# A decoder layer in split float32: one-hot gate rows built four tokens at a time, ScalarE scaling them, and three moves around it

## The chip, the core and the metric

The kernel runs on one core of a Trainium2 chip. A core has five engines that run side by side and hand tiles to each other by semaphores: TensorE (matmul, PE in the profile), VectorE (DVE), ScalarE (ACT), GpSimd (POOL) and SyncE (SP), which here issues most transfers. Each engine takes its instructions in the order in which they are written for it. The metric is the device time of one execution in microseconds; the time stated for a kernel is the median of its runs.

## The reference, cut to what matters

One decoder layer on 512 tokens of 2048 numbers: a projection, two kinds of windowed attention that are merged, a layer norm, then a product-key lookup (PEER) over 128 x 128 single-neuron experts, and a gated extra input.

```python
h1 = layer_norm(alpha * x + m @ w_out)
# PEER: 8 heads; each takes the 16 best of 128 x 128 experts by two half keys,
# expert index = i1 * 128 + i2, gate = softmax of the 16 scores
peer = sum over heads and picks of gate * gelu(h1 . u[expert]) * v[expert]
x = layer_norm(alpha * h1 + peer + sigmoid(h1 @ ple_gate) * (p @ ple_proj))
```

## The kernel before, in words

Every float32 matmul is made of three: operands are split into a rounded high half and a remainder, and `mm3` (lines 100 to 103) multiplies high by high, high by low and low by high. `load_split` (lines 87 to 98) brings in a weight chunk of 128 x 1024: SyncE loads `raw`, ScalarE copies the high half `whi` (line 93), VectorE subtracts to get the low half `wlo` (line 95; in places GpSimd, line 97). Each of the three has three buffers, and so the loads run at most three chunks ahead.

The order of the instructions on each engine is set when the kernel is built: a scheduler simulates the engines and emits what it believes to be ready first, within the dependencies and the buffers of each pool.

The stages that the change touches, in order:

- **Output projection and norm** (`mix`, line 459; `norm1`, line 483; driver, lines 515 to 523). `mix(0)` and `mix(1)` project two halves of 256 tokens, 32 steps each of 12 matmuls of 512 columns (`wo`). After four steps of `mix(1)` the norm of the first half, `norm1(0)`, is written in one piece: statistics, then 16 blocks in four groups, each block two transposes on TensorE (`ht`), a scaling on VectorE (line 502), a high half on ScalarE and a low half `m_lo` on VectorE (line 505). `spread` (lines 509 to 513) then lets GpSimd multiply and add the norm's weights over whole rows, in place, for the tiles `h1g` and `y1` that the transposes read.
- **Key search** (`half_keys`, line 635), interleaved with u columns (`dense_u`, line 712): 48 matmuls of 352 columns each (`hp`), a GELU, and a store to the DRAM tensor `ad`. 32 such columns (four groups of 8 experts) are made early by `look_units` (line 724).
- **Gates** (`dense_gates`, lines 654 to 679). For 352 tokens a 128 x 128 table of gates is the product of two one-hot matrices: VectorE compares an iota with the token's 16 x 8 first indices (`o1`, line 669) and second indices, scaled by the gate (`o2`, line 671), one token at a time; TensorE multiplies them into `pg` (line 673), ScalarE copies four tokens' result to `sg` (line 677), and `gd` in DRAM receives it. After each two groups of four tokens, a **step** (44 in all), `fill(1)` places one unit of other work: the last four u columns of the first 24, then 32 units of the extra input's gate (`ple_units`, line 681; 24 matmuls of 512 columns, chunk names `pg0_0` and so on). `gather_to` places the expert rows' work for the tokens done sparsely: a gather by GpSimd (line 599) and a row step on VectorE (line 606). The unit that closes each quarter of the extra input puts sigmoids into `psg` (line 706) and stores them to `base` by GpSimd's queue.
- **Eight more u columns**, then **gated groups** (loop at line 859). For the first four groups each of 8 values `a` (128 x 352) is loaded from `ad` by GpSimd's queue (line 866), multiplied by the gates `gl` (line 870), split into `ah` (line 873) and `al` (line 874) and used in 48 matmuls `vp`; the value half of the dense experts. Later groups compute `a` in place. The pool of `a` has two buffers.

`raw_p`, a load between key search and gates, holds one of the three `raw` buffers until `pj_lo` (line 781) has read it.

Of the kernel before, what the change touches and what calls it, by code (L numbers as in the profile page):

```python
# [9 lines left out]
F32 = mybir.dt.float32  # L10
# [3 lines left out]
AF = mybir.ActivationFunctionType  # L14
ALU = mybir.AluOpType
# [4 lines left out]
P = 128  # L20
# [7 lines left out]
TD = T - T0  # L28
# [12 lines left out]
def hybrid_layer(  # L41
# [26 lines left out]
    nc = tc.nc  # L68
# [12 lines left out]
    def bank(name, dt=F32):  # L81
        return pp.tile([P, 512], dt, tag="ps", name=name)
# [60 lines left out]
    op = s1.enter_context(tc.tile_pool(name="op", bufs=1))  # L143
# [156 lines left out]
    for c in range(2):  # L300
        ps = column_block(w_z[26 + c], xs, f"vb{c}")
# [181 lines left out]
    def norm1(half):  # L483
        for tb in (2 * half, 2 * half + 1):
            norm_stats(st[:, tb, :, :].rearrange("p a b -> p (a b)"), mv[:, tb, :])
            if tb % 2 == 0:
                nc.vector.tensor_scalar(y[tb], y[tb], mv[:, tb, 0:1], mv[:, tb, 1:2],
                                        op0=ALU.subtract, op1=ALU.mult)
            else:
                nc.vector.scalar_tensor_tensor(mv[:, tb, 2:3], mv[:, tb, 0:1], -1.0, mv[:, tb, 1:2],  # L490
                                               op0=ALU.mult, op1=ALU.mult)
                nc.scalar.activation(y[tb], y[tb], AF.Identity, bias=mv[:, tb, 2:3],
                                     scale=mv[:, tb, 1:2])
        yield
        hc = slice(half * 256, (half + 1) * 256)
        for kb in range(KB):
            ps = bank(f"ht{half}_{kb}")
            for i in range(2):
                nc.tensor.transpose(ps[:, i * P:(i + 1) * P],  # L499
                                    y[2 * half + i][:, kb * P:(kb + 1) * P], ident)  # L500
            t = xp.tile([P, 256], F32, tag="ht", name=f"ht{half}_{kb}")
            nc.vector.tensor_scalar(t, ps[:, 0:256], lnc[:, 0, kb:kb + 1], lnc[:, 1, kb:kb + 1],
                                    op0=ALU.mult, op1=ALU.add)
            nc.scalar.activation(hs[0][:, kb, hc], t, AF.Copy)
            nc.vector.tensor_sub(hs[1][:, kb, hc], t, hs[0][:, kb, hc])
            if kb % 4 == 3:
                yield
# [9 lines left out]
    rest = mix(1)  # L517
    for _ in range(4):
        next(rest)
    for _ in norm1(0):  # L520
        pass
    for _ in rest:
        pass

    pre_q = [load_split(w_q[0][:, u * 1024:(u + 1) * 1024], f"wq0_{u}") for u in range(2)]
# [3 lines left out]
    io = kp.tile([P, P], F32, name="io")  # L529
# [124 lines left out]
    def dense_gates(tb):  # L654
        i1, i2, gt = picks[tb]
        ps = bank(f"pit{tb}")
        for i, a in enumerate((i1, i2, gt)):
            nc.tensor.transpose(ps[:, i * P:(i + 1) * P], a, ident)
        tt = k3.tile([P, 3, P], F32, tag="tt", name=f"tt{tb}", bufs=2)
        nc.vector.tensor_copy(tt, ps[:, 0:384].rearrange("p (a t) -> p a t", t=P))  # L660
        for b in range(GX // 16 if tb == 1 else 0, 8):
            sg = k3.tile([P, P, 16], F32, tag="sg", name=f"sg{tb}_{b}", bufs=2)
            for t4 in range(4):
                ps = bank(f"pg{tb}_{b}_{t4}")
                t0 = b * 16 + t4 * 4
                for t1 in range(4):
                    t = t0 + t1
                    o1 = k3.tile([P, P], F32, tag="o1", name=f"o1_{tb}_{t}", bufs=8)
                    nc.vector.tensor_scalar(o1, io, tt[:, 0, t:t + 1], None, op0=ALU.is_equal)
                    o2 = k3.tile([P, P], F32, tag="o2", name=f"o2_{tb}_{t}", bufs=8)  # L670
                    nc.vector.tensor_scalar(o2, io, tt[:, 1, t:t + 1], tt[:, 2, t:t + 1],
                                            op0=ALU.is_equal, op1=ALU.mult)
                    nc.tensor.matmul(ps[:, t1 * P:(t1 + 1) * P], o1, o2, start=True, stop=True)  # L673
                if t4 % 2:
                    fill(1)
                    gather_to(steps[1] + 1)
                nc.scalar.activation(sg[:, :, t4 * 4:(t4 + 1) * 4].rearrange("p i t -> p t i"),
                                     ps.rearrange("p (t i) -> p t i", i=P), AF.Copy)
            nc.sync.dma_start(gdw[:, :, tb * 8 + b - T0 // 16, :], sg.rearrange("p (g i) t -> p g (i t)", i=GE))
# [43 lines left out]

    def look_units(i, pool, n, share):
        for i2 in range(i, i + n):
            a = pool.tile([P, TD], F32, tag="a", name=f"au{i2}")
            dense_u(i2, a, share())
            nc.sync.dma_start(ad[i2 // GE][:, i2 % GE, :], a)
            yield

    def fill(n):
        for _ in range(n):
            next(units, None)
# [24 lines left out]
    fpool = []  # L758
# [15 lines left out]
    k3 = s4.enter_context(tc.tile_pool(name="k3", bufs=2, side="right"))  # L774
# [8 lines left out]
    def gate_filler():  # L783
        yield from state["units"]
        yield from ple_units()

    units = gate_filler()
    for tb in range(1, NT):
        dense_gates(tb)
    fill(32 + LOOK * GE)  # L790
# [5 lines left out]
    ap2 = s5.enter_context(tc.tile_pool(name="ap2", bufs=2))  # L796
# [3 lines left out]
    def gather_steps():  # L800
        calls[0] += 1
        gather_to(calls[1] + calls[0] * (2 * HG + LEAD - calls[1]) // (NG * 8 + (NG - LOOK + 1) * 8 - 6))
# [56 lines left out]
    for g in range(NG):  # L859
        a_hi, a_lo = [], []  # L860
        if g:
            gt = gate_tile(g)
        for e in range(GE):
            a = ap2.tile([P, TD], F32, tag="a", name=f"a{g}_{e}")
            if g < LOOK:
                nc.gpsimd.dma_start(a, ad[g][:, e, :])
            else:
                dense_u(g * GE + e, a)
            a3 = a.rearrange("p (b t) -> p b t", t=16)
            nc.vector.tensor_mul(a3, a3, gt[:, :, e, :])  # L870
            h = ap2.tile([P, TD], F32R, tag="ah", name=f"ah{g}_{e}", bufs=GE + 1)
            l = ap2.tile([P, TD], F32R, tag="al", name=f"al{g}_{e}", bufs=GE + 1)
            nc.scalar.activation(h, a, AF.Copy)  # L873
            nc.vector.tensor_sub(l, a, h)  # L874
            a_hi.append(h)
            a_lo.append(l)
            if g >= LOOK:
                gather_steps()
        if g == NG - 1:
            lng = gp.tile([P, 2, D], F32, tag="slot_lo", name="lng")  # L880
            nc.sync.dma_start(lng, ln2.partition_broadcast(P))
            zs = gp.tile([P, NT - 1, D], F32, tag="slot_hi", name="zs")
            for tb in range(1, NT):
                lo_, hi_ = span[tb]
                z[tb] = zs[0:hi_ - lo_, tb - 1, :]
                nc.sync.dma_start(z[tb], base[tb][lo_:hi_, :])
        for c in range(8):
            ws = []
            for u in range(GE // 4):
                ws.append(load_split(v_dense[(g * 8 + c) * 2 + u], f"vd{g}_{c}_{u}"))  # L890
            for b in range(2):
                db = c * 2 + b
                ps = bank(f"vp{g}_{db}")
                for e in range(GE):
                    hi, lo = ws[e // 4]
                    o = (e % 4) * 256 + b * P
                    s = slice(o, o + P)
                    mm3(ps[:, :TD], hi[:, s], lo[:, s], a_hi[e], a_lo[e], e == 0, e == GE - 1)
                if g == 0:
                    nc.vector.tensor_copy(acc[:, db, :], ps[:, :TD])  # L900
                else:
                    nc.vector.tensor_add(acc[:, db, :], acc[:, db, :], ps[:, :TD])
            if g == NG - 1 and c % 2:
                for tb in range(1, NT):
                    ps = bank(f"zt{tb}_{c}")
                    lo_, hi_ = span[tb]
                    k = hi_ - lo_
                    for i in range(4):
                        nc.tensor.transpose(ps[:k, i * P:(i + 1) * P],
                                            acc[:, 2 * c - 2 + i, tb * P + lo_ - T0:tb * P + hi_ - T0], ident)  # L910
                    cs = slice(c // 2 * 512, c // 2 * 512 + 512)
                    nc.vector.tensor_add(z[tb][:, cs], z[tb][:, cs], ps[:k, :])
                    nc.vector.bn_stats(st2[:k, tb, c // 2, :], z[tb][:, cs])
            if g == NG - 1 and c >= 3:
                if c == 3:
                    finish_gathered()
            else:
                gather_steps()
# [115 lines left out]
```

## Time and profile before

| | us |
|---|---|
| median of 3 runs | 4023.78 (4021.25 to 4023.92) |
| the profiled execution's own time | 4021.22 |
| its span in the profile | 4019.4 |
| TensorE busy | 3822.7 (95%) |
| VectorE busy | 2704.3 (67%) |
| ScalarE busy | 1282.2 (32%) |
| GpSimd busy | 685.3 (17%) |

The mean granted TensorE clock of this execution is 0.976 of full speed. Matmuls overlap, so their lengths add up to more than the time they take: the distance from one start to the next is the cost. "Idle before" in a group's row is the time its engine stood still just before the group's instructions, and the releaser is what ended it.

### The profile page before, as it was taken

How to read it: one execution, taken by the hardware profiler on the slowest of the kernel's cores; microseconds unless marked ns; L12 is line 12 of the kernel's file. 1: busy time of each engine (PE TensorE's matmuls, PEld its weight loads, DVE VectorE, ACT ScalarE, POOL GpSimd, SP SyncE). 2: the span in 40 equal slices, each digit the busy share in tenths (PEclk: the TensorE clock that was granted, in tenths of full speed). 3: DMA queues.
4: the chain of work that ended last, by engine and by line, in shares of the span. 5: the costliest groups of instructions: out<-in, count | busy, mean ns of one | idle time of the engine just before them, and what ended most of it. 6: DMA issues, size and time to landing. Idle time of an engine off the chain costs nothing.

```text
span 4019.4 us, 54040 instructions
## 1 busy us (share of the span) xinstructions
PE 3822.7 (95%) x21545; PEld 3535.9 (88%) x21545; DVE 2704.3 (67%) x4220; ACT 1282.2 (32%) x1660; POOL 685.3 (17%) x493
## 2 busy tenths in 40 slices
PE   8999999999998889979988899999999999999996
PEld 7888877888886789978878898999999999999996
DVE  5344343222257788899996777777777777777877
ACT  3222233222233433334433222333333333333331
POOL 0000000000002355521122222222211211111110
PEclk9999999999999999989998999999999999999998
DMA  4222222222256455658888787888888888888884
GB/s 141 95 89 85 76 74 71 92 95 94 95 190 191 155 163 181 226 199 281 287 292 303 270 304 287 304 324 310 302 323 303 310 316 298 316 310 306 318 300 152
DMA packets 242941, 886.99 MB, mean 221 GB/s; under 512 B 23040, under 2 KB 76416, under 8 KB 198016
## 3 DMA queue, kind: packets, MB, share of 16 engines
q1 hardware_dynamic: 182672, 499.91, 36.8%
q0 software_dynamic: 52672, 375.15, 25.5%
q10 hardware_dynamic: 7344, 8.47, 0.6%
q8 instruction: 169, 2.77, 0.3%
q14 instruction: 84, 0.69, 0.1%
HBM read 841.24 MB, written 41.42 MB: 220 GB/s over the span
## 4 chain that ended last, share of the span: by engine, by line
PE 81%; DVE 11%; DMA 3%; issue 3%; ACT 1%; POOL 1%; POOLq 0%; DVEq 0%; ACTq 0%; SPq 0%
PE hp L101 8%; PE hp L103 8%; PE hp L102 8%; PE vp L101 7%; PE vp L103 7%; PE vp L102 7%; PE ps_g L101 3%; PE ps_g L102 3%; PE ps_g L103 3%; PE pg L673 2%; DVE row L606 2%; PE pg L101 1%; PE pg L102 1%; PE pg L103 1%; DMA a<-ad 1%
## 5 line engine op out<-in xcount | busy, mean ns | idle before, releaser
L101 PE MATMUL vp<-ah,whi_vd 128*128 128x352 f32 x2048 | 657.5, 327 | 29.1 <-ACT ah L873 18.2
L103 PE MATMUL hp<-m_hi,wlo_u 128*128 128x352 f32 x2048 | 665.2, 325 | 20.4 <-DVE wlo_u L95 13.6
L101 PE MATMUL hp<-m_hi,whi_u 128*128 128x352 f32 x2048 | 668.4, 326 | 0.0
L102 PE MATMUL hp<-m_lo,whi_u 128*128 128x352 f32 x2048 | 662.5, 323 | 0.0
L102 PE MATMUL vp<-al,whi_vd 128*128 128x352 f32 x2048 | 662.1, 325 | 0.3 <-DVE al L874 0.3
L103 PE MATMUL vp<-ah,wlo_vd 128*128 128x352 f32 x2048 | 644.7, 326 | 9.8 <-DVE wlo_vd L95 9.8
L93 ACT ACTIVATE whi_vd<-raw_vd 128x1024 fp32r<-128x1024 f32 x256 | 270.4, 1059 | 671.5 <-PE vp L102 469.7
L93 ACT ACTIVATE whi_u<-raw_u 128x1024 fp32r<-128x1024 f32 x256 | 271.0, 1059 | 525.6 <-PE hp L102 309.1
L101 PEld LDWEIGHTS vp<-ah,whi_vd 128*128 128x128 f32 x2048 | 387.8, 191 | 33.6 <-ACT ah L873 20.1
L95 DVE TENSOR_TENSOR wlo_vd<-raw_vd,whi_vd 128x1024 fp32r<-128x1024 f32 x256 | 312.5, 1221 | 142.6 <-ACT whi_vd L93 142.3
L95 DVE TENSOR_TENSOR wlo_u<-raw_u,whi_u 128x1024 fp32r<-128x1024 f32 x236 | 295.3, 1252 | 165.6 <-ACT whi_u L93 164.9
L103 PEld LDWEIGHTS hp<-m_hi,wlo_u 128*128 128x128 f32 x2048 | 386.3, 189 | 22.4 <-DVE wlo_u L95 15.3
L103 PEld LDWEIGHTS vp<-ah,wlo_vd 128*128 128x128 f32 x2048 | 385.5, 190 | 11.2 <-DVE wlo_vd L95 11.2
L102 PEld LDWEIGHTS hp<-m_lo,whi_u 128*128 128x128 f32 x2048 | 390.1, 190 | 0.0
L102 PEld LDWEIGHTS vp<-al,whi_vd 128*128 128x128 f32 x2048 | 388.4, 190 | 0.9 <-DVE al L874 0.8
L101 PEld LDWEIGHTS hp<-m_hi,whi_u 128*128 128x128 f32 x2048 | 388.0, 189 | 0.0
L599 POOL DMA_INDIRECT row<-in_u_rows,eidx x160 | 204.1, 1276 | 816.6 <-DVE row L606 546.8
L599 POOL DMA_INDIRECT row<-in_v_rows,eidx x160 | 193.3, 1208 | 829.7 <-DVE accg L620 648.3
L620 DVE SCALAR_TENSOR_TENSOR accg<-row,act,accg 128x2048 f32<-128x2048 f32 x128 | 300.3, 2346 | 0.4
L606 DVE SCALAR_TENSOR_TENSOR row<-row,h1g 128x2048 f32<-128x2048 f32 x128 | 293.4, 2300 | 0.0
L511 POOL TENSOR_TENSOR h1g<-h1g,lnb 128x2048 f32<-128x2048 f32 x1 | 4.6, 4619 | 1259.5 <-PE ht L499 1259.5
L101 PE MATMUL ps_g<-x_hi,whi_g 128*128 128x512 f32 x512 | 202.9, 396 | 0.0
(332 smaller groups left out, 7387.4 us busy)
## 6 DMA issues: line engine op xcount, KB each, us to landing
raw_u<-in_u_dense SPq DMA_DIRECT2D x256, 512.0 KB, 5.5
raw_vd<-in_v_dense SPq DMA_DIRECT2D x256, 512.0 KB, 5.6
raw_g<-in_w_z SPq DMA_DIRECT2D x64, 512.0 KB, 3.4
raw_wo<-in_w_out SPq DMA_DIRECT2D x64, 512.0 KB, 4.2
raw_wq<-in_w_q SPq DMA_DIRECT2D x64, 512.0 KB, 4.0
gd<-sg SPq DMA_DIRECT2D x22, 1024.0 KB, 7.9
gl<-gd POOLq DMA_DIRECT2D x16, 1408.0 KB, 9.7
raw_pg<-in_w_gate SPq DMA_DIRECT2D x32, 512.0 KB, 5.4
```

Of the source, the lines that this page charges most:

```text
L93: nc.scalar.activation(hi[:, :n], raw[:, :n], AF.Copy)
L95: last_lo[0] = nc.vector.tensor_sub(lo[:, :n], raw[:, :n], hi[:, :n])
L101: nc.tensor.matmul(ps, whi, mhi, start=start, stop=False, **kw)
L102: nc.tensor.matmul(ps, whi, mlo, start=False, stop=False, **kw)
L103: nc.tensor.matmul(ps, wlo, mhi, start=False, stop=stop, **kw)
L511: nc.gpsimd.tensor_mul(o, o, lnb[:, 0, :])
L599: nc.gpsimd.indirect_dma_start(out=row, out_offset=None, in_=u_rows if n < HG else v_rows, in_offset=bass.IndirectOffsetOnAxis(ap=eidx[:, ...
L606: nc.vector.scalar_tensor_tensor(row, row, 1.0, state["h"][n >= HK], op0=ALU.mult, op1=ALU.mult, accum_out=act[:, n:n + 1])
L620: nc.vector.scalar_tensor_tensor(o, row, act[:, k:k + 1], o, op0=ALU.mult, op1=ALU.add)
L673: nc.tensor.matmul(ps[:, t1 * P:(t1 + 1) * P], o1, o2, start=True, stop=True)
```

## The change

It has four parts. In `dense_gates` one compare now makes the one-hot rows of four tokens (128 x 512, two tensor operands read with repeats) for the first indices and one for the second, two buffers each, where a token had two instructions of 128 x 128; the scaling by the gate becomes one ScalarE instruction per token. `fill(4)` ahead of the gates places the four remaining u columns between key search and gates, so that the steps start with the extra input's units. The pool of `a` gets four buffers for the loaded and the gated values. In the driver, `norm1(0)` is advanced by one group after every third step of `mix(1)`.

```diff
--- before.py
+++ after.py
@@ -517,9 +517,12 @@
     rest = mix(1)
     for _ in range(4):
         next(rest)
-    for _ in norm1(0):
-        pass
-    for _ in rest:
+    early = norm1(0)
+    next(early)
+    for n, _ in enumerate(rest):
+        if n % 3 == 2:
+            next(early, None)
+    for _ in early:
         pass
 
     pre_q = [load_split(w_q[0][:, u * 1024:(u + 1) * 1024], f"wq0_{u}") for u in range(2)]
@@ -663,14 +666,20 @@
             for t4 in range(4):
                 ps = bank(f"pg{tb}_{b}_{t4}")
                 t0 = b * 16 + t4 * 4
+                def onehot(row, name):
+                    eq = k3.tile([P, 4, P], F32, tag=name, name=f"{name}{tb}_{t0}", bufs=2)
+                    nc.vector.tensor_tensor(
+                        eq, tt[:, row, t0:t0 + 4].unsqueeze(2).to_broadcast([P, 4, P]),
+                        io.unsqueeze(1).to_broadcast([P, 4, P]), op=ALU.is_equal)
+                    return eq
+
+                o1 = onehot(0, "o1")
+                eq = onehot(1, "eq")
                 for t1 in range(4):
                     t = t0 + t1
-                    o1 = k3.tile([P, P], F32, tag="o1", name=f"o1_{tb}_{t}", bufs=8)
-                    nc.vector.tensor_scalar(o1, io, tt[:, 0, t:t + 1], None, op0=ALU.is_equal)
                     o2 = k3.tile([P, P], F32, tag="o2", name=f"o2_{tb}_{t}", bufs=8)
-                    nc.vector.tensor_scalar(o2, io, tt[:, 1, t:t + 1], tt[:, 2, t:t + 1],
-                                            op0=ALU.is_equal, op1=ALU.mult)
-                    nc.tensor.matmul(ps[:, t1 * P:(t1 + 1) * P], o1, o2, start=True, stop=True)
+                    nc.scalar.activation(o2, eq[:, t1, :], AF.Copy, scale=tt[:, 2, t:t + 1])
+                    nc.tensor.matmul(ps[:, t1 * P:(t1 + 1) * P], o1[:, t1, :], o2, start=True, stop=True)
                 if t4 % 2:
                     fill(1)
                     gather_to(steps[1] + 1)
@@ -723,7 +732,7 @@
 
     def look_units(i, pool, n, share):
         for i2 in range(i, i + n):
-            a = pool.tile([P, TD], F32, tag="a", name=f"au{i2}")
+            a = pool.tile([P, TD], F32, tag="a", name=f"au{i2}", bufs=4 if pool is not fpool[0] else 2)
             dense_u(i2, a, share())
             nc.sync.dma_start(ad[i2 // GE][:, i2 % GE, :], a)
             yield
@@ -785,6 +794,7 @@
         yield from ple_units()
 
     units = gate_filler()
+    fill(4)
     for tb in range(1, NT):
         dense_gates(tb)
     fill(32 + LOOK * GE)
@@ -861,7 +871,7 @@
         if g:
             gt = gate_tile(g)
         for e in range(GE):
-            a = ap2.tile([P, TD], F32, tag="a", name=f"a{g}_{e}")
+            a = ap2.tile([P, TD], F32, tag="a", name=f"a{g}_{e}", bufs=4)
             if g < LOOK:
                 nc.gpsimd.dma_start(a, ad[g][:, e, :])
             else:
```

Three places of the order, each engine's instructions as they are issued (the numbers at the ends of names tell instances apart).

VectorE at the end of the key search, before (`ix` is the lookup's result, `tt` the transposed indices and gates, `o1_1_32` and `o2_1_32` the rows of token 32 of block 1):

```order
L579 TENSOR_REDUCE ix_8815<-oh3_3_0_13295 128x32
L579 TENSOR_REDUCE ix_8815<-oh3_3_1_13299 128x32
L660 COPY tt1_13335<-pit1_13331 128x384
L669 TENSOR_SCALAR o1_1_32_13339<-io_8811,tt1_13335 128x128
L671 TENSOR_SCALAR o2_1_32_13341<-io_8811,tt1_13335 128x128
L669 TENSOR_SCALAR o1_1_33_13344<-io_8811,tt1_13335 128x128
L671 TENSOR_SCALAR o2_1_33_13346<-io_8811,tt1_13335 128x128
```

and with the change (`wlo_pg0` are low halves of the extra input's first units, `row9` to `row11` row steps):

```order
L582 TENSOR_REDUCE ix_8815<-oh3_3_0_13295 128x32
L582 TENSOR_REDUCE ix_8815<-oh3_3_1_13299 128x32
L95 TENSOR_TENSOR wlo_pg0_0_13636<-raw_pg0_0_13633,whi_pg0_0_13635 128x1024
L609 SCALAR_TENSOR_TENSOR row9_13092,act_7404<-row9_13092,h1g_7423 128x2048
L790 TENSOR_TENSOR pj_lo_13326<-raw_p_13327,pj_hi_13325 128x1024
L95 TENSOR_TENSOR wlo_pg0_1_13705<-raw_pg0_1_13702,whi_pg0_1_13704 128x1024
L609 SCALAR_TENSOR_TENSOR row10_13239,act_7404<-row10_13239,h1g_7423 128x2048
L663 COPY tt1_13591<-pit1_13587 128x384
L95 TENSOR_TENSOR wlo_pg0_2_13776<-raw_pg0_2_13773,whi_pg0_2_13775 128x1024
L609 SCALAR_TENSOR_TENSOR row11_13663,act_7404<-row11_13663,h1g_7423 128x2048
L671 TENSOR_TENSOR o11_32_13595<-tt1_13591,io_8811 128x512
L671 TENSOR_TENSOR eq1_32_13597<-tt1_13591,io_8811 128x512
```

The lookup was followed by `tt` and the one-hot rows; now three low halves, `pj_lo` and three row steps stand in that place, and two compares follow them. Earlier in the lookup, five low halves of u columns have come in, which these rows don't show.

GpSimd's queue around the second gated group, before (`a1_0` is value 0 of group 1, `gl1` its gates):

```order
L866 DMA a0_7_17545<-ad_7401 128x352
L866 DMA a1_0_18093<-ad_7401 128x352
L599 DMA row67_17817<-in_u_rows,eidx_7403 128x2048
L853 DMA gl1_18091<-gd_7400 128x2816
L866 DMA a1_1_18100<-ad_7401 128x352
L599 DMA row68_17820<-in_u_rows,eidx_7403 128x2048
L599 DMA row69_17887<-in_u_rows,eidx_7403 128x2048
L599 DMA row70_17954<-in_u_rows,eidx_7403 128x2048
L866 DMA a1_2_18107<-ad_7401 128x352
```

and with the change:

```order
L876 DMA a1_0_17741<-ad_7401 128x352
L876 DMA a1_1_17748<-ad_7401 128x352
L876 DMA a1_2_17755<-ad_7401 128x352
L863 DMA gl1_17739<-gd_7400 128x2816
L602 DMA row66_17398<-in_u_rows,eidx_7403 128x2048
L876 DMA a1_3_17762<-ad_7401 128x352
L602 DMA row67_17465<-in_u_rows,eidx_7403 128x2048
L876 DMA a1_4_17769<-ad_7401 128x352
L602 DMA row68_17468<-in_u_rows,eidx_7403 128x2048
L602 DMA row69_17535<-in_u_rows,eidx_7403 128x2048
L602 DMA row70_17602<-in_u_rows,eidx_7403 128x2048
L602 DMA row71_17669<-in_u_rows,eidx_7403 128x2048
```

Values `a1_1` and `a1_2` have moved ahead of the gates and of the gathers, which follow in a row; `a1_5` comes after the last of these.

VectorE at the end of the first half's norm, before (`st` is the other half's statistics):

```order
L95 TENSOR_TENSOR wlo_wo1_1_2_8367<-raw_wo1_1_2_8364,whi_wo1_1_2_8366 128x1024
L505 TENSOR_TENSOR m_lo_7361<-ht0_10_8207,m_hi_7360 128x256
L481 BN_STATS st_7431<-y3_7426 128x6
L505 TENSOR_TENSOR m_lo_7361<-ht0_11_8214,m_hi_7360 128x256
L505 TENSOR_TENSOR m_lo_7361<-ht0_12_8221,m_hi_7360 128x256
L502 TENSOR_SCALAR ht0_13_8228<-ht0_13_8225,lnc_7427 128x256
L502 TENSOR_SCALAR ht0_14_8235<-ht0_14_8232,lnc_7427 128x256
L502 TENSOR_SCALAR ht0_15_8242<-ht0_15_8239,lnc_7427 128x256
L95 TENSOR_TENSOR wlo_wo1_1_3_8385<-raw_wo1_1_3_8382,whi_wo1_1_3_8384 128x1024
L95 TENSOR_TENSOR wlo_wo1_1_4_8403<-raw_wo1_1_4_8400,whi_wo1_1_4_8402 128x1024
L505 TENSOR_TENSOR m_lo_7361<-ht0_13_8228,m_hi_7360 128x256
```

and with the change:

```order
L505 TENSOR_TENSOR m_lo_7361<-ht0_12_8447,m_hi_7360 128x256
L502 TENSOR_SCALAR ht0_13_8454<-ht0_13_8451,lnc_7427 128x256
L95 TENSOR_TENSOR wlo_wo1_1_6_8411<-raw_wo1_1_6_8408,whi_wo1_1_6_8410 128x1024
L505 TENSOR_TENSOR m_lo_7361<-ht0_13_8454,m_hi_7360 128x256
L502 TENSOR_SCALAR ht0_14_8461<-ht0_14_8458,lnc_7427 128x256
L502 TENSOR_SCALAR ht0_15_8468<-ht0_15_8465,lnc_7427 128x256
L95 TENSOR_TENSOR wlo_wo1_1_7_8429<-raw_wo1_1_7_8426,whi_wo1_1_7_8428 128x1024
L505 TENSOR_TENSOR m_lo_7361<-ht0_14_8461,m_hi_7360 128x256
L505 TENSOR_TENSOR m_lo_7361<-ht0_15_8468,m_hi_7360 128x256
L95 TENSOR_TENSOR wlo_wo1_2_0_8485<-raw_wo1_2_0_8482,whi_wo1_2_0_8484 128x1024
L95 TENSOR_TENSOR wlo_wo1_2_1_8503<-raw_wo1_2_1_8500,whi_wo1_2_1_8502 128x1024
```

The scalings of blocks 13 to 15, whose transposes are the last readers of `h1g` and `y1`, stood between the low halves of chunks 2 and 3 of the quarter; now they stand between those of chunks 5 and 7.

## Rows read from the trace of the kernel before

**Rows 1.** Page, part 1: each engine's busy time, share of the span, instructions.

```profile
PE 3822.7 (95%) x21545; PEld 3535.9 (88%) x21545; DVE 2704.3 (67%) x4220; ACT 1282.2 (32%) x1660; POOL 685.3 (17%) x493
```

**Rows 2.** Table of stretches; columns in its first line.

```profile
core 0: us, PE busy (x) PEld busy (x) DVE busy (x) ACT busy (x) POOL busy (x), PEclk, DMA share, GB/s
1778.00:1800.00 22.00, 21.21 (x121) 20.90 (x122) 17.46 (x52) 8.77 (x9) 1.00 (x1) 0.82 0.48 147
...
1850.00:2050.00 200.00, 189.63 (x991) 161.35 (x990) 179.09 (x463) 79.82 (x84) 29.31 (x35) 0.97 0.86 280
2050.00:2142.00 92.00, 78.55 (x384) 67.29 (x383) 85.50 (x239) 37.12 (x38) 21.54 (x17) 0.81 0.82 283
...
2200.00:2460.00 260.00, 225.43 (x1314) 219.64 (x1315) 189.12 (x239) 72.21 (x88) 64.66 (x68) 0.95 0.77 285
2460.00:3938.00 1478.00, 1475.34 (x9185) 1475.00 (x9184) 1144.99 (x1064) 485.10 (x577) 286.81 (x236) 1.00 0.85 310
```

**Rows 3.** TensorE's waits: waiting line, releaser: us in total, times, longest.

```profile
PE vp L101 <- ACT ah L873: 18.2, 6, 5.0
PE wo L102 <- DVE wlo_wo L95: 14.5, 4, 13.0
```

**Rows 4.** Timelines near 1777 and in the tail: start us, length us.

```profile
1768.77 1.24 DVE L574 TENSOR_TENSOR oh<-bcf,io 128x512 f32<-128x512 f32 x2
...
1777.17 0.29 DVE L669 TENSOR_SCALAR o<-io,tt 128x128 f32<-128x128 f32 x1
1777.37 0.34 DVE L671 TENSOR_SCALAR o<-io,tt 128x128 f32<-128x128 f32 x1
1777.63 0.28 DVE L669 TENSOR_SCALAR o<-io,tt 128x128 f32<-128x128 f32 x1
...
1777.77 1.70 PE L673 MATMUL pg<-o,o 128*128 128x128 f32 x6 [24.36 <-DVE o L671]
...
2093.73 1.28 PE L673 MATMUL pg<-o,o 128*128 128x128 f32 x10
```

**Rows 5.** Groups by line, VectorE 1753 to 2142, POOL 1753 to 2460.

```profile
L606 DVE SCALAR_TENSOR_TENSOR row<-row,h1g 128x2048 f32<-128x2048 f32 x45 | 102.5, 2281 | 0.0
L95 DVE TENSOR_TENSOR wlo_pg<-raw_pg,whi_pg 128x1024 fp32r<-128x1024 f32 x32 | 39.0, 1218 | 9.9 <-ACT whi_pg L93 9.8
...
L599 POOL DMA_INDIRECT row<-in_u_rows,eidx x86 | 108.0, 1255 | 461.2 <-DVE row L606 229.3 <-DVE o L669 217.5 <-DMA a<-ad 10.2
```

**Rows 6.** Page, DMA issues (us to landing); tile `a`, 2190 to 2470.

```profile
a<-ad POOLq DMA_DIRECT2D x32, 176.0 KB, 5.2
...
base<-psg POOLq DMA_DIRECT2D x16, 256.0 KB, 7.3
...
L870 DVE TENSOR_TENSOR a<-a,gl x32: 512/518/527, 2203.5 to 2447.2; 128x352 f32<-128x352 f32 x32
...
  DMA a<-ad: 33.9, 8
...
  POOL a L866: 32.2, 17
```

**Rows 7.** Groups by line and shape, ScalarE, whole span.

```profile
L677 ACT ACTIVATE sg<-pg 128x512 f32<-128x512 f32 x88 | 92.3, 1075 | 109.1 <-PE pg L673 108.9
...
L260 ACT ACTIVATE p<-p,nm 128x128 f32<-128x128 f32 x32 | 12.4, 387 | 0.0
...
L706 ACT ACTIVATE psg<-pg 128x512 f32<-128x512 f32 x16 | 9.4, 605 | 30.2 <-DMA base<-psg 18.6 <-DVE o L671 8.5 <-PE pg L103 2.6
...
L585 ACT ACTIVATE gt<-gt 128x128 f32<-128x128 f32 x3 | 0.9, 304 | 6.7 <-DVE gt L584 6.7
```

**Rows 8.** VectorE's timeline after 1260; POOL's groups, 1255 to 1285.

```profile
1263.35 3.13 DVE L95 TENSOR_TENSOR wlo_wo<-raw_wo,whi_wo 128x1024 fp32r<-128x1024 f32 x1
...
1271.76 8.74 DVE L505 TENSOR_TENSOR m_lo<-ht,m_hi 128x256 fp32r<-128x256 f32 x2
...
L511 POOL TENSOR_TENSOR h1g<-h1g,lnb 128x2048 f32<-128x2048 f32 x1 | 4.6, 4619 | 1259.5 <-PE ht L499 1259.5
```

## Prediction

> **What bounds the kernel now.** The page comes first: TensorE is busy 95% of the span [rows 1], so a change can only win back time that TensorE loses. The table by stretches says where that is: the idle time of a stretch, plus what the granted clock takes (one minus the clock, times the length). In the long stretch from 2460 on nothing is lost: 9185 matmuls of 352 columns in 1478 us, 0.161 us apart [rows 2]. That row is also the price of a u column, 48 such matmuls or 7.7 us. The change touches five other places [rows 2 to 4]:
> - the norm, near 1280: one wait of 13.0 us
> - the step from key search to gates: one wait of 24.4 us, then in 1778 to 1800 0.8 idle and 0.18 x 22 = 4.0 of clock, so 29
> - the gates, 1850 to 2050: 10.4 idle and 0.03 x 200 = 6, so 16
> - the gates' tail, 2050 to 2142: 13.5 idle and 0.19 x 92 = 17.5, so 31
> - the first gated groups, 2200 to 2460: 34.6 idle and 0.05 x 260 = 13, so 48
>
> The list of waits names the causes of the first and the last: a low half of `wo`, late from VectorE, and the gated values' high half `ah`, 18.2 us in six waits [rows 3].
>
> **Key search to gates.** TensorE stands still because VectorE is sorting and looking up keys and makes its first one-hot row only at 1777.2 [rows 4]. `fill(4)` puts four u columns, 4 x 7.7 = 31 us, into this hole, so TensorE ends them at about 1753.4 + 30.8 = 1784. They aren't free: their low halves go through the same VectorE queue. More than before there now stand, ahead of the first one-hot matmul: five of these (1.2 us each [rows 5]), three of the ple units, `pj_lo` (like one of them), two row steps of 2.3 [rows 5] (three stand there, but one has only moved out of the search) and two of the new compares (1.2): 6.0 + 3.6 + 1.2 + 4.6 + 1.2 = 17 after 1777, so 1794. One of the ple chunks must also wait for the slot that `raw_p` holds until `pj_lo` has run, and for its load (5.2 us in the nearest row, for a third of the bytes [rows 6]), which could make it 1801. The gap left is 10 to 17 us, I take 14; with the clock's 4 the place loses 18, not 29. **Gain 11** (5 to 20: from the late load with a longer stretch at half clock, to a gap of 5).
>
> **The compares.** Today a token costs 0.46 us of VectorE: two instructions whose starts stand 0.20 and 0.26 apart [rows 4]; eight tokens, one step of the filler, cost 3.7. The new instruction has 512 elements a row and two tensors. The nearest row is the lookup's compare of the same size, two in 1.24 us [rows 4], so about 0.60 each. A step becomes 4 x 0.60 = 2.4. With a row step (2.3) and a low half (1.2) VectorE falls from 7.2 to 5.9 us a step, against 7.4 of TensorE: a ple unit is 24 matmuls of 512 columns (0.161 x 512 / 352 = 0.234, so 5.6), and a token is two one-hot records at 0.11 (ten in 1.28 us [rows 4]). Over 352 tokens VectorE saves 352 x 0.46 - 176 x 0.60 = 56 us. Most of that lay beside TensorE's work: it can return only the 16 us lost in 1850 to 2050. **Gain 6** (0 to 13): the slack rises from 0.2 to 1.5 us a step, but the bursts of row steps stay.
>
> ScalarE takes on 352 scalings. No row has this form. A 128x128 without a column operand takes 304 ns, one with a bias column 387 [rows 7]; where such instructions follow each other they overlap by at most some 0.1. I take 0.29, from the row with one column operand; the ends are 0.22 and 0.39. That is 102 us (77 to 137) on an engine that is busy 32% [rows 1]; in a step it makes 2.3 beside a high half of about 1.06 and two `sg` copies of 1.07 [rows 7], 5.5 of 7.4 us. While units fill the steps this is covered; where that cover is gone it sets the pace, next.
>
> **The tail.** Four units have left the filler, so by TensorE's order twelve steps, 24 groups of four tokens, now run bare, where eight did. Over the last 16 steps TensorE has 4 x 5.6 + 32 x 0.9 = 51 us of work. VectorE has 64 compares (38), some 15 row steps (35) and a few low halves and sums (11), 84 in all; and where no row steps are left ScalarE leads, 4 x 0.29 + 1.07 and the hand-over, near 2.5 us a group. 84 to 98 less 51 is 33 to 47; with 39 against the 31 before it is **8 lost** (2 to 15).
>
> **Gated values.** A value's round trip through an `a` buffer is 0.6 to issue, 5.2 to land, and a multiply, a high half and a low half of about 0.52 each [rows 6]: 7.3 us. Two buffers give one value per 3.7 us. TensorE wants one per 24 matmuls, 3.9 us. Nothing is left for a gather (1.26 [rows 5]) ahead of the load in POOL's queue, or a row step (2.3) ahead of the multiply; and the multiply that waits for its load, 33.9 us in eight waits [rows 6], keeps the low halves of `vd` behind it on VectorE. Four buffers give one per 1.8 us. The first group can't profit fully, as its last values are stored just before; and POOL now issues up to six gathers ahead of a group's sixth value. I leave 22 of the 48. **Gain 26** (10 to 40: only the longest waits shortened, or all but the first group's).
>
> **The norm.** The 13.0 us wait [rows 3] is VectorE held by POOL: once the last transpose has read `h1g` and `y`, POOL runs four tensor operations of 4.6 us and more, and meanwhile a low half takes 3.13 us, and two `m_lo` take 8.74 [rows 8]. Spread, the transposes end some 14 us later, POOL starts at about 1275, and VectorE then has `wlo_wo1_1_7`, two `m_lo` and `wlo_wo1_2_0` to pass: 3.1 + 8.7 + 4.6 = 16.4, against two units of 12 matmuls in hand, 5.6. It is the same wait of 11 to 13, only later. **0** (a gain of 3 to a loss of 3).
>
> **Sum.** 11 + 6 - 8 + 26 + 0 = 35 less than the profiled execution's 4021.2, so 3986. The runs' median lies 2.6 above that execution; against it, 3988. A difference under 0.2%, 8 us, can't be told from none.
>
> **A rule that speaks against it.** The trace holds two-tensor VectorE operations only while POOL computes [rows 8]; beside POOL's gathers low halves and row steps keep a mean of 1.22 and 2.28 [rows 5]. The Trainium skill (GPSIMD Engine Reference, section Specifications) says that POOL shares its SBUF interfaces with VectorE and contends with VectorE instructions that have two SBUF inputs, and makes no exception for gathers. By that rule the new compares, which have two tensors where the old had one, join what POOL can hold; it is the last rival, and would give 4011.
>
> **Rivals.**
> - *The loads are not what the groups wait for.* POOL works in order, and its gathers wait for row buffers; then a deeper `a` ring is filled no sooner. For it: six gathers stand ahead of the sixth value. Against it: in 17 places POOL waited for a reader of an `a` buffer, 32.2 us [rows 6]. Only some 0 to 5 of the 26 would come: about 4010. Chance 0.15.
> - *The norm's wait does go*, if the low halves of `wo` pass before POOL starts: 3986 - 13 = 3973. Against it is the queue above. Chance 0.10.
> - *ScalarE in order, and slower.* Sigmoids into `psg` have waited 18.6 us for that buffer's store [rows 7], 1.2 each of 16, with little that was urgent behind them. Now scalings stand behind them, and VectorE can be only two groups ahead, with two buffers each of `o1` and `eq`. If a sigmoid waits the whole 7.3 us of a store [rows 6], half a step (3.7) is covered and 3.6 lands on TensorE: 16 x 3.6 = 58. Without the gates' 6 that is 4021 - 11 - 26 + 8 + 58 = 4050. It decides from 16 x 2.3 = 37 us on, a mean wait of 6; the row's is a fifth of that. Chance 0.09.
> - *The compares are held by POOL's gathers.* Some 45 of 1.26 us [rows 5] lie in the gates, 15 of them in the tail. Held for all of them, VectorE's slack is used up (the 6 gone) and the tail is longer by 15 x 1.26 = 19: 3986 + 6 + 19 = 4011. Chance 0.04, as no row beside a gather shows it.
>
> **How the numbers follow.** The forecast has 0.62. Faster by over 0.2%: the forecast, the norm's 0.10 and half of the first rival's, 0.80. Slower: 0.08, nearly all of ScalarE's case. The rest, 0.12, is within 0.2%. The terms' ends, taken as independent, make about 25 either way, 3963 to 4013; the norm's rival takes the lower end to 3957, and the loads' and compares' rivals, at 4011 with ends of their own, the upper to 4018.
>
> **What would show it.** Right: the wait for one-hot rows after the search falls from 24 to between 10 and 17 and names ScalarE; four u columns run in 1753 to 1784; the tail's idle time grows; the multiply of the gated groups hardly waits for `a`, and TensorE's loss there about halves; a wait of 11 to 13 stands near 1290, behind POOL's tensor operations. Wrong: `wo` without a long wait; `a` waited for as before; compares well over 0.7 long; ScalarE waiting for `base` with TensorE behind it.

## The result and the profile after

| | before | changed |
|---|---|---|
| median | 4022.52 us (4 runs) | 3966.65 us (4 runs, 3965.0 to 3971.3) |
| ratio | 1 | 0.9867, 95% interval 0.985 to 0.9884 |
| profiled execution, span | 4019.4 us | 3969.3 us |

The change is 56 us faster by the medians, 50 by the two profiled executions. The forecast was 3988, with a range from 3957 to 4018: the direction and the range held, the gain was 60% larger than the sum of 35.

The page's first line, against [rows 1]: TensorE works 16 us less and ScalarE 93 more.

```profile
PE 3807.1 (96%) x21545; PEld 3524.3 (89%) x21545; DVE 2662.6 (67%) x3692; ACT 1375.6 (35%) x2012; POOL 686.8 (17%) x493
```

To compare stages, both traces are cut at the same matmuls: the first `wo` of the second half, the last of `wo`, the last key score, the 12th one-hot product, 2050, the last one-hot product, the first `vp`, the first `vp` of the fifth group, the last `vp`. The columns are those of [rows 2]. Before:

```profile
1234.80:1345.60 110.80, 95.74 (x417) 76.44 (x416) 76.54 (x89) 43.49 (x52) 22.66 (x10) 0.94 0.63 196
1345.60:1752.80 407.20, 367.47 (x2657) 363.73 (x2656) 353.68 (x1002) 146.05 (x210) 227.38 (x96) 0.96 0.56 181
1752.80:1792.60 39.80, 14.65 (x79) 14.10 (x78) 34.85 (x115) 9.32 (x12) 0.94 (x1) 0.66 0.39 132
1792.60:2050.00 257.40, 247.03 (x1339) 214.52 (x1338) 232.88 (x597) 105.84 (x113) 38.07 (x43) 0.97 0.87 287
2050.00:2141.30 91.30, 77.85 (x381) 66.59 (x379) 85.50 (x239) 36.70 (x37) 21.54 (x17) 0.81 0.82 285
2141.30:2204.60 63.30, 58.32 (x366) 58.03 (x364) 39.81 (x36) 22.39 (x27) 14.70 (x12) 0.98 0.89 328
2204.60:2558.30 353.70, 323.73 (x1921) 317.94 (x1922) 261.17 (x313) 103.14 (x125) 81.62 (x81) 0.96 0.78 289
2558.30:3988.00 1429.70, 1425.46 (x8871) 1424.53 (x8870) 1113.07 (x1039) 465.17 (x550) 267.83 (x222) 1.00 0.83 304
```

and after:

```profile
1234.60:1344.60 110.00, 95.42 (x416) 75.82 (x415) 79.02 (x89) 43.65 (x52) 22.65 (x10) 0.95 0.64 198
1344.60:1755.30 410.70, 369.52 (x2657) 365.06 (x2656) 361.28 (x1002) 146.54 (x210) 226.08 (x96) 0.95 0.56 179
1755.30:1810.40 55.10, 44.10 (x253) 41.73 (x252) 44.98 (x103) 25.28 (x44) 3.77 (x3) 0.88 0.63 217
1810.40:2050.00 239.60, 239.60 (x1273) 203.94 (x1272) 195.18 (x237) 160.37 (x335) 44.07 (x43) 1.00 0.87 290
2050.00:2126.90 76.90, 50.21 (x267) 44.96 (x266) 62.41 (x82) 58.40 (x135) 17.05 (x15) 0.80 0.87 306
2126.90:2190.60 63.70, 58.84 (x369) 58.55 (x367) 40.13 (x37) 22.48 (x27) 13.53 (x13) 0.99 0.89 328
2190.60:2508.50 317.90, 313.01 (x1920) 310.07 (x1921) 259.31 (x313) 103.26 (x124) 82.09 (x79) 0.99 0.87 321
2508.50:3938.00 1429.50, 1425.44 (x8873) 1424.35 (x8872) 1113.38 (x1039) 465.51 (x550) 267.04 (x222) 1.00 0.84 304
```

The first column but one is the length of a stage. The norm took 110.8 and takes 110.0; the key search, which the change leaves as it was, 3.5 more; from the last key score to the last one-hot product it was 388.5 and is 371.6, 16.9 less; from there to the first `vp` it is 0.4 more; the first four gated groups took 353.7 and take 317.9, 35.8 less; the long rest is the same to 0.2. So the whole gain lies in two places. Between 1810 and 2050 TensorE is now busy without a break, where 10.4 us were idle; the tail has 26.7 us idle in place of 13.5.

The waits of TensorE, against [rows 3] and the 24.4 us of [rows 4]:

```profile
PE pg L682 <- ACT o L681: 21.5, 11, 11.0
PE pg L682 <- DVE o L671: 14.8, 7, 3.4
PE wo L102 <- DVE wlo_wo L95: 13.5, 5, 11.7
PE vp L101 <- ACT ah L883: 4.9, 1, 4.9
```

The longest wait for a one-hot row fell from 24.4 to 11.0 and now ends with ScalarE's scaling; `wo` still waits 11.7 at once (13.5 in all); the gated values' `ah` is waited for once.

The compares, by line with the shortest, median and longest duration (ns), and the scalings by group:

```profile
L671 DVE TENSOR_TENSOR o<-tt,io x88: 678/685/694, 1796.3 to 2120.7; 128x512 f32<-128x512 f32 x88
L671 DVE TENSOR_TENSOR eq<-tt,io x88: 677/685/714, 1796.9 to 2120.1; 128x512 f32<-128x512 f32 x88
```

```profile
L681 ACT ACTIVATE o<-eq,tt 128x128 f32<-128x128 f32 x352 | 113.5, 388 | 40.0 <-PE pg L682 30.7 <-DVE eq L671 9.2
```

A compare of 512 takes 685 ns and never more than 714, with 43 of POOL's gathers issued in that stretch: the 97 compares that run beside such an issue have a mean of 685 ns, the 73 beside no POOL instruction 688. This speaks against the Trainium skill's rule that was weighed (GPSIMD Engine Reference, Specifications: contention with VectorE instructions that have two SBUF inputs) as far as gathers go. The scaling takes 388 ns, what the row with one column operand had [rows 7].

The multiply's waits for a load, against [rows 6]:

```profile
  DMA a<-ad: 5.8, 5
```

33.9 us in eight waits became 5.8 in five. And the norm, VectorE's timeline, against [rows 8]:

```profile
1275.70 5.00 DVE L95 TENSOR_TENSOR wlo_wo<-raw_wo,whi_wo 128x1024 fp32r<-128x1024 f32 x1
1280.62 9.43 DVE L505 TENSOR_TENSOR m_lo<-ht,m_hi 128x256 fp32r<-128x256 f32 x2
1289.98 6.65 DVE L95 TENSOR_TENSOR wlo_wo<-raw_wo,whi_wo 128x1024 fp32r<-128x1024 f32 x2
```

One low half of 5.00, two `m_lo` of 9.43 together: the same hold, 12 us later.

### The profile page after: what moved, and what is told of

It reads as the page before. It is cut to its first block, busy times and chain, and to the rows that moved or that the text cites. A ratio compares the mean times of both kernels' runs of the same rounds, so it can differ in the third digit from the quotient of the medians.

```text
span 3969.3 us, 54078 instructions
## 1 busy us (share of the span) xinstructions
PE 3807.1 (96%) x21545; PEld 3524.3 (89%) x21545; DVE 2662.6 (67%) x3692; ACT 1375.6 (35%) x2012; POOL 686.8 (17%) x493
## 4 chain that ended last, share of the span: by engine, by line
PE 85%; DVE 9%; DMA 3%; issue 1%; ACT 1%; POOL 0%; POOLq 0%; DVEq 0%; ACTq 0%
PE vp L103 8%; PE vp L101 8%; PE vp L102 8%; PE hp L103 8%; PE hp L101 8%; PE hp L102 7%; PE ps_g L101 3%; PE ps_g L102 3%; PE ps_g L103 3%; PE pg L101 2%; PE pg L103 2%; PE pg L102 2%; PE pg L682 1%; PE wo L102 1%; PE wo L103 1%
```

## The experiments

Each ratio is to the kernel before on the same chip. Runs that are set against each other were in part on different chips, so that their ratios compare them better than their medians. The four with `alone` in their name hold one part of the change each.

**onehot_alone**: only `dense_gates` as in the change.

> Only the compares of four tokens and ScalarE's scaling. Theory: the gates' stage was limited by VectorE, so the 16 us lost between 1850 and 2050 shrink to under 3, and the tail, with 8 bare steps, loses about 25 in place of 31; the wait after the key search stays at 24 to 25. In all 15 to 22 us faster than before, 4000 to 4008. Rival: the gates' gain came from the moved u columns, not from the compares; then 10 or more of the 16 us stay and the time is within 8 us of before.

4032.49 us, ratio 1.0025 (1.0012 to 1.0038): slower, against both theories. In the stretch 1850 to 2045 TensorE is idle 19.2 us, where it was 10.4 before. The new kernel's row, and the only line of TensorE's waits in this stretch before:

```profile
1850.00:2045.00 195.00, 175.85 (x916) 149.53 (x915) 142.55 (x175) 117.82 (x245) 30.11 (x33) 0.95 0.83 271
...
PE pg L673 <- DVE o L671: 10.4, 2, 5.5
```

It stands still twice, 10.0 and 9.2 us. The first of them, in the timelines of ScalarE, POOL, VectorE and TensorE:

```profile
1875.77 1.20 ACT L712 ACTIVATE psg<-pg 128x512 f32<-128x512 f32 x2
...
1892.68 0.60 ACT L712 ACTIVATE psg<-pg 128x512 f32<-128x512 f32 x1 [8.27 <-DMA base<-psg]
1893.18 1.26 ACT L678 ACTIVATE o<-eq,tt 128x128 f32<-128x128 f32 x4
...
1884.62 0.60 POOL L715 DMA_DIRECT2D base<-psg  x1 [1.13 <-ACT whi_pg L93]
...
1888.41 0.69 DVE L668 TENSOR_TENSOR o<-tt,io 128x512 f32<-128x512 f32 x1
...
1883.16 0.38 PE L658 MATMUL pit<-ident,ix 128*128 128x128 f32 x2
1883.37 0.27 PE L658 MATMUL pit<-ident,gt 128*128 128x128 f32 x1
1893.62 2.50 PE L679 MATMUL pg<-o,o 128*128 128x128 f32 x10 [9.98 <-ACT o L678]
```

A unit that closes a quarter of the extra input makes four sigmoids into two `psg` buffers. The third waits until the first store, issued by POOL at 1884.6, has landed, 8.27 us of ScalarE's time, and the scalings of the next tokens stand behind it: that is the rival that ended on the slow side. It costs so much because of what TensorE does at 1883.16: with this unit a token block ends, `pit` transposes the next block's indices, and no row of that block can exist before. VectorE's first compare of the new block runs only at 1888.4, behind sums of the closing unit, a low half and a row step, so some 6 of the 10 us are VectorE's queue, as in the kernel before, and some 4 are the sigmoid's. The closing units come at steps 12 and 28 (four u columns and 8 or 24 units), and the blocks of 96, 128 and 128 tokens end at steps 12 and 28. The two waits of the kernel before, 5.5 us at 1890.6 and 4.8 at 2027.1, stand at the same two places.

**fill_alone**: only `fill(4)`.

> Only the four u columns ahead of the gates, with the old compares. Theory: the wait after the key search falls from 24 to about 11, some 13 to 15 us, but four more steps run bare with the dear compares (3.7 us a step), so the tail's loss grows from 31 to 45 to 55: within 8 us of before, or up to 10 slower. Rival: the gates' loss in 1850 to 2050 was due to the u columns among the units and goes with them: then about 4010.

4018.92 us, ratio 0.9995 (0.9986 to 1.0004): no difference, as the theory said. But where the gates were expected to lose as before, nothing is lost:

```profile
1850.00:2045.00 195.00, 195.00 (x1026) 165.53 (x1025) 180.93 (x444) 82.24 (x85) 34.02 (x38) 1.00 0.87 294
```

So the gates' gain came not from the compares. It may come, as this rival had it, from the u columns that are gone, or from the place of the closing units: the four columns moved out shift these to steps 8, 16, 24 and 32, clear of the changes of block. The wait after the search fell to 10.0, and the tail's loss grew: from 2050 to the last one-hot product 24.7 us are idle in place of 13.5, at a clock of 0.72 in place of 0.81.

**onehot_fill1** tells the two apart: compares as in onehot_alone, and `fill(1)`, a shift by one step (the edit, against onehot_alone).

```diff
     units = gate_filler()
+    fill(1)
```

> The compares and ScalarE's scaling on the kernel before, and one u column ahead of the gates in place of none. Theory: the two waits of 9 to 10 us of the compares alone are there because a closing unit of the extra input ends exactly where the next token block's indices are transposed; one column ahead shifts the closing units by one step and both waits go: TensorE's loss in the gates falls from 25 to under 9, and the time from 4032 to 4008 to 4018. Rival: the scalings queue behind the sigmoids that wait for their store wherever these fall: the gates still lose 20 or more, above 4024.

4017.04 us, ratio 0.9994 (0.9984 to 1.0005), 15 us below onehot_alone. Both long waits are gone, with three of the four columns still among the units, so it is the place and not the columns; the longest wait left in this stretch is 1.7 us:

```profile
1850.00:2045.00 195.00, 191.77 (x998) 162.04 (x997) 152.90 (x186) 122.61 (x251) 33.60 (x36) 1.00 0.86 293
```

**no_onehot**: the change with the old compares.

> The change without its compares: the four u columns, the four buffers and the spread norm, with the old compares of VectorE. Theory: with the closing units of the extra input no longer falling on a change of the token block, the cheap compares are worth some 10 us in gates and tail (TensorE's loss 6 and 38 with them, 12 and 42 without): 3974 to 3982. Rival: the compares are worth nothing or less, as when they were tried alone: 3968 or below.

3978.74 us, ratio 0.9892 (0.9877 to 0.9907), 12 us above the change by the medians, 10 by the ratios, whose intervals just overlap. From the last key score to the last one-hot product it takes 381.1 us (1751.7 to 2132.8), the change 371.6. So the compares are worth some 10 us once the closing units are out of the way. All of it lies behind 2045: the wait after the search is 9.9 here and 11.0 in the change, and from there to 2045 TensorE has no idle time in either.

**ring_alone**: only `bufs=4` for `a`.

> Only four buffers for the gated values. Theory: all of the gain of the first four gated groups comes from this, 30 to 38 us: 3985 to 3993, with TensorE's loss in these groups near 11 in place of 46. Rival: part of it came from the new order of the rows that the earlier parts bring (gathers and row steps stand elsewhere): then under 20 us, above 4003.

3984.78 us, ratio 0.9907 (0.9891 to 0.9923), 37 us: this is most of the change. The first four groups take 320.8 us in place of 353.7. The multiply's waits:

```profile
  DMA a<-ad: 6.6, 5
```

Where the two buffers cost is seen at the start of the second group (2276.1 before, 2256.4 in the change). POOL's loads of its last values, two lines of them left out before, and then the change:

```profile
2272.88 0.59 POOL L866 DMA_DIRECT2D a<-ad  x1 [1.10 <-DVE al L874]
...
2284.36 0.58 POOL L866 DMA_DIRECT2D a<-ad  x1 [0.97 <-DVE al L874]
...
2297.45 0.57 POOL L866 DMA_DIRECT2D a<-ad  x1
...
2253.63 1.69 POOL L876 DMA_DIRECT2D a<-ad  x3 [1.09 <-DVE al L884]
```

Before, the last five values come in three rounds, the first two begun when `al` has freed a buffer, and TensorE's waits in the first four groups all lie in the first half of a group's 384 matmuls. With four buffers the last three values come in one round, ahead of the group.

**ring3**: the change with three buffers.

```diff
-            a = ap2.tile([P, TD], F32, tag="a", name=f"a{g}_{e}", bufs=4)
+            a = ap2.tile([P, TD], F32, tag="a", name=f"a{g}_{e}", bufs=3)
... (the same in look_units)
```

> The whole change with three buffers for the gated values in place of four. Theory: what counts is how many round trips of a load stand in a row at a group's start, three pairs with two buffers, one with four; three buffers leave two, so TensorE's loss in the first four groups lies between 11 and 55, at 20 to 35: 3974 to 3991. Rival: any buffer beyond two is enough, as the loads then overlap the multiplies: 3963 to 3972.

3984.01 us, ratio 0.9911 (0.9897 to 0.9925), 17 us above the change, between two buffers and four as expected. The first four groups take 332.9 us, with 16.2 idle where the change has 317.9 and 4.9. The multiply's waits:

```profile
  DMA a<-ad: 28.3, 6
```

**norm_alone**: only the spread.

> Only the spread of the first half's norm. Theory: the wait near 1283 only moves by some 12 us and stays 11 to 13 long: 4019 to 4026, no difference. Rival: the spread does gain what the wait near 1283 was, 10 us or more: under 4013.

4021.91 us, ratio 1.0 (0.9992 to 1.0009): nothing.

**pieces**: the change, and POOL's norm work cut.

```diff
-        nc.gpsimd.tensor_mul(o, o, lnb[:, 0, :])
-        nc.gpsimd.tensor_add(o, o, lnb[:, 1, :])
+        for c in range(0, D, 512):
+            cs = slice(c, c + 512)
+            nc.gpsimd.tensor_mul(o[:, cs], o[:, cs], lnb[:, 0, cs])
+            nc.gpsimd.tensor_add(o[:, cs], o[:, cs], lnb[:, 1, cs])
```

> The whole change, with GpSimd's multiply and add of the norm weights cut into four pieces of 512 columns each. Theory: VectorE's two-tensor instructions get through one per GpSimd operation, so four times as many and shorter operations hold each for 1.2 us in place of 4.6: the wait of 11.7 us near 1295 falls under 4, and the same holds for the second pair of rows during the key search: 10 to 25 us off, 3942 to 3957. Rival: VectorE is held as long in all, whatever the size: within 4 us of the change, 3963 to 3971.

3959.02 us, ratio 0.9847 (0.9834 to 0.9861), 7.6 below the change by the medians, with intervals that overlap, and 17.5 by the profiled executions (spans 3951.8 and 3969.3), of which the change's is the slowest of its four and this one the fastest of its five: the median is short of the 10 that the theory asked for. VectorE, POOL and TensorE near 1270:

```profile
1265.51 2.20 DVE L95 TENSOR_TENSOR wlo_wo<-raw_wo,whi_wo 128x1024 fp32r<-128x1024 f32 x1
1267.63 4.38 DVE L505 TENSOR_TENSOR m_lo<-ht,m_hi 128x256 fp32r<-128x256 f32 x3
...
1268.82 1.48 POOL L514 TENSOR_TENSOR h1g<-h1g,lnb 128x512 f32<-128x512 f32 x1
...
1282.03 0.50 PE L102 MATMUL wo<-wlo_wo,m_hi 128*128 128x512 f32 x1 [3.43 <-DVE wlo_wo L95]
```

Three `m_lo` now take 4.38 where two took 9.43, one per POOL piece of about 1.5, and the wait of 11.7 is 3.4. The norm's stage is 104.7 us long (110.0 in the change), the key search 399.8 (410.7). So the mechanism held; its size in the medians lies below the forecast.

**look4**: the change, with four of the eight u columns that follow the gates made into units.

```diff
-            state["units"] = look_units(0, fpool[0], (LOOK - 1) * GE, lambda: sq_open[0])
+            state["units"] = look_units(0, fpool[0], (LOOK - 1) * GE + 4, lambda: sq_open[0])
...
-    for _ in look_units((LOOK - 1) * GE, ap2, GE, lambda: False):
+    for _ in look_units((LOOK - 1) * GE + 4, ap2, GE - 4, lambda: False):
```

> The whole change, with four of the eight u columns that follow the gates made into units of the gates, so that 8 steps and not 12 run bare. Theory: the tail's loss comes with the bare steps, 38 us over 12, so it falls by 9 to 15: 3952 to 3959. Rival: the loss is VectorE's and ScalarE's work, the same whichever units stand there, and the four columns that are missing after the gates uncover the load of the first gates `gl`: 3964 or above.

3970.31 us, ratio 0.9877 (0.9861 to 0.9892): no gain, and not for the rival's reason. The tail does lose less, 15.3 us idle from 2050 on in place of 26.7. But four columns put the closing units back on steps 12 and 28, and the two waits came back, 8.43 and 8.60. The first, ScalarE's sigmoid and then TensorE:

```profile
1904.11 0.60 ACT L715 ACTIVATE psg<-pg 128x512 f32<-128x512 f32 x1 [6.72 <-DMA base<-psg]
...
1896.35 0.27 PE L661 MATMUL pit<-ident,gt 128*128 128x128 f32 x1
1905.05 1.23 PE L682 MATMUL pg<-o,o 128*128 128x128 f32 x4 [8.43 <-ACT o L681]
```

**look4_hole**: the same four columns, but placed ahead of the gates (`fill(8)`), which leaves the steps as in the change.

> The whole change with four of the eight later u columns moved ahead of the gates too: eight columns there in place of four, and the same units at the same steps. Theory: the wait of 11 us for the first one-hot row is VectorE's work, so 31 us more of matmuls cover it, less the low halves that come with them: TensorE's loss there falls from 14 to under 7, the tail stays at 38: 3955 to 3963. Rival: the added low halves push the row work back as far as the columns reach, and the start of the first gated group is uncovered: 3965 or above.

3964.36 us, ratio 0.9871 (0.9855 to 0.9886), not distinguishable from the change, and between the theory's range and the rival's. The wait after the search fell from 11.0 to 5.8,

```profile
PE pg L682 <- ACT o L681: 5.8, 1, 5.8
```

and the first gated group waits 7.6 where it waited 4.9: half of the gain is given back there.

**look3_pieces** and **look5_pieces**: pieces, with three or five of those columns among the units.

> The change with GpSimd's norm work in four pieces and three of the eight later u columns among the gates' units. Theory: with three columns the closing units of the extra input end one step ahead of a change of the token block, so the two waits of 8 to 9 us that four columns brought are under 3 each; nine bare steps in place of twelve cost 8 to 12 less in the tail. With the pieces: 3942 to 3952. Rival: any units that go on longer in the gates bring the sigmoids' waits: 3957 or above.

3959.2 us, ratio 0.986 (0.9844 to 0.9876): no faster than pieces, a miss. The long waits at the changes of block are away (1.7 at most in 1850 to 2045), and the tail does lose less. Its last 16 steps in pieces, and here:

```profile
2013.90:2109.60 95.70, 69.66 (x366) 61.59 (x365) 78.28 (x101) 69.72 (x159) 23.49 (x19) 0.82 0.85 293
...
2038.50:2132.90 94.40, 74.79 (x391) 65.16 (x390) 76.93 (x100) 70.17 (x161) 19.09 (x17) 0.86 0.84 288
```

Idle time and clock are 26.0 + 0.18 x 96 = 43 us there and 19.6 + 0.14 x 94 = 33 here: 10 less, as the theory had it. But from the last key score to the first `vp` it is 431.7 us against 432.7, so that nearly all of it was lost again on the way: 2.6 us of idle time in 1850 to 2045 and some 3 of clock in the gates, and some 2 behind them. These are not the two long waits of the rival; where they come from is open.

> The same with five columns: the closing units end one step after a change of the token block, and seven steps run bare. Theory: waits at the closing units stay under 3 us, as the new block's rows already run ahead, and the tail loses 15 to 20 less than in the change: 3934 to 3946. Rival: right after a change of the block VectorE has no lead, so the waits of 8 us come back, and three columns uncover the first gated group: 3952 or above.

3937.8 us, ratio 0.9799 (0.9786 to 0.9813): the fastest of all, 2% below the kernel before, 29 us below the change and 21 below pieces. The closing units end at steps 13 and 29, one behind the changes of block. From 1793 to 2050 TensorE has no idle time, and the tail has 14.4 us in place of 26.7:

```profile
1741.00:1793.30 52.30, 43.41 (x270) 42.83 (x269) 43.02 (x100) 24.97 (x41) 0.94 (x1) 0.93 0.59 195
1793.30:2050.00 256.70, 256.70 (x1420) 224.16 (x1419) 209.78 (x250) 171.01 (x359) 42.97 (x45) 1.00 0.90 301
2050.00:2129.80 79.80, 65.43 (x344) 57.32 (x343) 63.68 (x82) 57.21 (x130) 16.74 (x15) 0.89 0.86 298
```

## Why the prediction was right, and where its steps were not

- **Key search to gates**, 11 forecast. The wait is 11.0 (14 taken, 10 to 17 given), ends at 1798 (1794 to 1801 given) and ends with ScalarE. The stage's idle time fell from 25.2 to 11.0, 14 us: right, a little small.
- **The compares**, 6 forecast in 1850 to 2050. The prices were right (0.60 apart, scaling 0.29 apart), the step was wrong: "it can return only the 16 us lost in 1850 to 2050" took these 16 for the price of VectorE's compares. The idle 10.4 of them were two waits at two changes of block, where the first compare comes late because other work stands ahead of it; `fill(4)` removed them, as fill_alone, onehot_fill1 and look4 show together, by shifting the closing units. The compares alone make them longer. What the compares return, some 10, lies in the tail. So the gates gave back all of the 16, not 6, and for search, gates and tail together 16.9 came where 11 + 6 - 8 = 9 were forecast.
- **The tail**, 8 lost forecast. Idle time and clock are 26.7 + 0.20 x 77 = 42 against 13.5 + 0.19 x 91 = 31: 11 lost, inside 2 to 15.
- **Gated values**, 26 forecast, 36 measured in the stage and 37 by ring_alone. "TensorE wants one per 24 matmuls, 3.9 us" was wrong: a group has 384 matmuls, 48 for each of its eight values, and the loop uses all eight in its first sum, with three matmuls each. By the mean rate two buffers, one value per 3.7 us, would have been enough for 48 matmuls, 7.7 us. What counts, as the loads at the start of the second group show, is how many round trips stand in a row when a group begins; by the mean rate three buffers would have been enough too, and ring3 still lies between. The size was put too low by that step, which left 22 of 48; 5 of idle time and 3 of clock are left.
- **The norm**, 0 forecast, 0.8 measured, and 1.0 as a ratio alone: the wait moved by 12 us, as its queue said.
- **The rivals.** The slow one, with a chance of 0.09, was real as a mechanism: 8.27 us of waiting for one `psg` buffer, with scalings behind it. Its bound, "It decides from 16 x 2.3 = 37 us on, a mean wait of 6", missed that two waits in the right place do. In the change sigmoids still wait for that store, 16.2 us in seven waits, 14.0 of them before 2010, where TensorE has no idle time. That they don't reach it comes from where `fill(4)` puts the closing units, which the prediction did not look at: that is luck. Loads that don't matter, a norm's wait that goes, and compares held by gathers: none showed.

Of the 56 us, then, 37 are the buffers, and the rest is the four columns together with the compares: alone the one gives nothing measurable and the other loses 10. Without the four buffers, both also made the first four groups some 8 us longer (362 against 353.7 in either trace), which used up the 7 us by which fill_alone reaches the first `vp` sooner after the search; why is not settled.

## What to carry to other kernels

Before an idle stretch is put down to the engine that it waits for, look at where in the program it comes: two waits at two block ends are a matter of alignment, and moving a few units by one step can be worth more than making the work cheaper. Work moved to an in-order engine stands behind everything that this engine waits for, so list its longest waits before giving it something urgent. And count buffers by the round trips in a row at the point of first use, not by a mean rate.

## What the runs showed of the hardware that was not expected

Two-tensor instructions of VectorE pass one for each tensor operation of POOL in both sizes that were run: with pieces of 512 columns, about 1.5 us each, three `m_lo` took 4.38 us, where behind whole rows, 4.6 us and more each, two took 9.43. Beside POOL's issue of gathers the same kind of instruction is not held: the compares that overlapped one took 685 ns in the mean, those that overlapped no POOL instruction 688.
